# Layer 2's gated feed-forward blocks 5 to 21 as seven half-size products instead of eight

## The chip, the cores and the metric

The kernel runs on one core of a Trainium2 chip. Five engines matter: TensorE (PE) multiplies, with its weight loads shown apart as PEld; VectorE (DVE), ScalarE (ACT) and GpSimd (POOL) work on elements; SyncE (SP) issues the transfers. Each engine takes its instructions in the order in which they stand in its queue. The metric is the device time of the core in microseconds, as the median of several runs.

## The reference

A sequence of 512 tokens with 1024 features passes through two blocks, each with two layers. The change touches only the first block, and there only the second layer (l = 1), whose sublayers are a gated feed-forward (ffn1), a mixer of four kinds of heads, and another gated feed-forward (ffn2). Cut to that:

```python
D_MODEL = 1024; SEQ = 512; DEPTH = 2; D_FF = 2816

def swiglu(h, w13, w2):
    a, b = jnp.split(h @ w13, 2, axis=-1)
    return (jax.nn.silu(a) * b) @ w2

for l in range(DEPTH):
    mod = (cond @ ada_w[l] + ada_b[l]).reshape(B, N_SUBLAYERS, 3, 1, D)
    h = adaln_pre(x, norm_g[l, 0], mod[:, 0, 0], mod[:, 0, 1])
    x = x + 0.5 * mod[:, 0, 2] * swiglu(h, ffn1_w13[l], ffn1_w2[l])
    ...
    h = adaln_pre(x, norm_g[l, 2], mod[:, 2, 0], mod[:, 2, 1])
    x = x + 0.5 * mod[:, 2, 2] * swiglu(h, ffn2_w13[l], ffn2_w2[l])
```

Then the second block (a spatial gating unit, differential attention and a convolutional feed-forward, twice) follows.

## The kernel before

Activations lie with features on the 128 partitions and the 512 tokens along the free axis: the residual is eight tiles `xs[d]` of 128x512. Each float32 operand of a product is split into a rounded part hi (a cast on ACT) and the rest lo (a subtraction), and `mm3` (L397) makes three matmuls of each step: hi by hi, hi by lo, lo by hi.

**Weights.** A list of units, made in the order of use by the planner (`plan_ffn`, L263), is loaded by `load` (L318) into one of three `raw` buffers of 128x2048. `split_one` (L329) turns half a unit (1024 columns, eight steps of K) into a tile `w` of a pool of five: one cast on ACT (L345), then four subtractions of 256 columns on POOL (L348). The products of the adaptive norm (`ada` units) also go through this list, but they are two DVE instructions each (L339, 128x1024). `next_w` (L391) takes a finished tile and calls `pump` (L359), which splits ahead until two tiles are ready. In ffn1 of layer 2, eight ada units stand among blocks 3 to 8: one behind block 3, two behind 4, one behind 5, two behind 6, one each behind 7 and 8. In ffn2 there are none.

**A feed-forward** (`ffn`, L667) has 22 blocks of 128 hidden features. For each block `project` (L717) multiplies twice, gate and value, 24 matmuls of 512 columns each; ACT takes silu of the gate, DVE multiplies by the value out of PSUM (L688), and `hilo` (L412 to L416) splits the result: cast on ACT, lo on DVE. The blocks go in two portions (`HALVES`, L21): after 12 and after the other 10, `out_phase` (L560) multiplies them by w2, eight outputs of 36 or 30 matmuls with two weight tiles each, and `x_add` (L554) adds each output to the residual. The last two outputs of the last portion are joined with the next norm in `seam` (L597), in two halves of the tokens.

PSUM has a pool of five general tiles (`pt`) and three for products (`pd`).

## Time and profile before

| | |
|---|---|
| median of three runs | 3350.55 us (3347.01 to 3351.17) |
| profiled execution, its own time | 3353.2 us |
| its span | 3351.4 us |
| mean granted TensorE clock | 0.989 |
| PE busy | 3252.3 us, 97% |
| DVE, ACT, POOL busy | 46%, 38%, 51% |
| layer 2's ffn1 blocks | from about 1142 us |
| layer 2's ffn2 blocks | from about 1861 us |

The profile is one execution on the chip: start and length of every instruction, what its engine waited for before it, and the chain of work that ended last. Busy shares are averages over the whole span; a single stage is read from the windows, timelines and waits of that stage.

### The profile page before, as it was taken

Reading aid. Unit: us, or ns where it says so; the run is one execution under the profiler, and the core shown is the slowest. Engines: PE = TensorE matmul, PEld = TensorE weight load, DVE = VectorE, ACT = ScalarE, POOL = GpSimd, SP = SyncE. Lnnn points to the kernel's source line nnn. Section 1 sums busy time; section 2 is a strip of 40 time slices with the busy share of each in tenths; the row PEclk is TensorE's granted clock in tenths of the full one; section 3 lists DMA queues with packets and bytes.
Section 4 is the critical chain, followed back from the end, with each engine's and each line's share of the span. In section 5 each row is a group of like instructions: output and inputs, shape, how many; then the busy total and the mean of one; then the engine's idle time right before and its main releaser. Section 6 shows DMA issues by size and latency. Waiting matters only on the chain.

```text
span 3351.4 us, 45142 instructions
## 1 busy us (share of the span) xinstructions
PE 3252.3 (97%) x17498; PEld 2690.2 (80%) x17498; DVE 1531.5 (46%) x2918; ACT 1282.6 (38%) x2127; POOL 1725.9 (51%) x2205
## 2 busy tenths in 40 slices
PE   6999999999999999999999999999999999999998
PEld 4878877678888888887778888887888887788887
DVE  6425377655333421137765221166452437654143
ACT  4222354443222422236344322355442335644242
POOL 5656562135566655556213655554465655355553
PEclk9999999999999999999999999999999999999999
DMA  6546323124454443232202222222132222222322
GB/s 251 196 165 237 113 101 103 64 78 174 167 213 165 145 153 111 78 122 91 91 27 88 101 91 102 81 97 81 64 107 95 96 93 82 67 89 90 107 87 65
DMA packets 72238, 379.18 MB, mean 113 GB/s; under 512 B 7566, under 2 KB 10126, under 8 KB 41560
## 3 DMA queue, kind: packets, MB, share of 16 engines
q1 hardware_dynamic: 72008, 376.28, 32.6%
q8 instruction: 138, 2.26, 0.3%
q14 instruction: 76, 0.62, 0.1%
q10 hardware_dynamic: 16, 0.02, 0.0%
HBM read 369.96 MB, written 6.31 MB: 112 GB/s over the span
## 4 chain that ended last, share of the span: by engine, by line
PE 74%; DVE 5%; ACT 2%; issue 0%; POOL 0%; DMA 0%; DVEq 0%; ACTq 0%; POOLq 0%
PE p L402 21%; PE p L401 21%; PE p L403 21%; PE p L1166 1%; PE p L1541 1%; PE po L1769 1%; PE p L729 1%; PE p L728 1%; PE p L727 1%; PE p L1524 1%; ACT w L345 0%; DVE rt L1639 0%; DVE qk L1640 0%; DVE qk L1641 0%; DVE pp L1749 0%
## 5 line engine op out<-in xcount | busy, mean ns | idle before, releaser
L348 POOL TENSOR_TENSOR w<-raw,w 128x256 fp32r<-128x256 f32 (+1 forms) x2128 | 1687.0, 824 | 1566.2 <-ACT w L345 1418.2
L401 PE MATMUL p<-hi,w 128*128 128x512 f32 (+1 forms) x4400 | 1649.6, 375 | 17.0 <-ACT hi L170 13.3
L402 PE MATMUL p<-lo,w 128*128 128x512 f32 (+1 forms) x4400 | 1640.6, 373 | 2.4 <-DVE lo L485 2.2
L403 PE MATMUL p<-hi,w 128*128 128x512 f32 (+1 forms) x4400 | 1636.2, 372 | 1.0 <-POOL w L383 1.0
L401 PEld LDWEIGHTS p<-hi,w 128*128 128x128 f32 x4400 | 833.2, 189 | 167.5 <-ACT hi L170 16.0
L402 PEld LDWEIGHTS p<-lo,w 128*128 128x128 f32 x4400 | 832.7, 189 | 152.9 <-issue 5.6
L403 PEld LDWEIGHTS p<-hi,w 128*128 128x128 f32 x4400 | 832.4, 189 | 146.2 <-issue 3.9
L345 ACT CAST w<-raw 128x1024 fp32r<-128x1024 f32 (+3 forms) x580 | 552.8, 956 | 866.1 <-PE p L403 725.3
L339 DVE SCALAR_TENSOR_TENSOR raw<-raw,cond 128x1024 f32<-128x1024 f32 x144 | 202.4, 1436 | 188.9 <-DMA raw<-in_ada_dram 181.6
L688 DVE TENSOR_TENSOR s<-s,p 128x512 f32<-128x512 f32 x88 | 60.3, 686 | 398.6 <-PE p L403 394.0
L556 DVE SCALAR_TENSOR_TENSOR x<-p,gate,x 128x512 f32<-128x512 f32 (+1 forms) x92 | 62.5, 679 | 337.1 <-PE p L403 337.1
L416 DVE TENSOR_TENSOR lo<-s,hi 128x512 fp32r<-128x512 f32 x132 | 126.2, 956 | 99.6 <-ACT hi L415 99.5
L696 DVE SCALAR_TENSOR_TENSOR cv<-p,cols,cv 128x511 f32<-128x511 f32 x88 | 65.6, 749 | 209.8 <-ACT cv L170 209.8
L415 ACT CAST hi<-s 128x512 fp32r<-128x512 f32 x132 | 81.6, 618 | 191.5 <-DVE s L688 135.1
L170 ACT ACTIVATE cv<-p,cols 128x512 f32<-128x512 f32 x88 | 68.3, 780 | 211.6 <-PE p L403 211.5
L170 ACT ACTIVATE s<-p 128x512 f32<-128x512 f32 x88 | 52.5, 597 | 212.8 <-PE p L403 212.8
L558 DVE TENSOR_TENSOR x<-p,x 128x512 f32<-128x512 f32 (+1 forms) x56 | 34.4, 615 | 208.2 <-PE p L403 208.2
L431 DVE TENSOR_TENSOR ss<-ss,sq 128x512 f32<-128x512 f32 (+1 forms) x97 | 65.2, 672 | 60.6 <-ACT sq L170 59.7
L170 ACT ACTIVATE sq<-x 128x512 f32<-128x512 f32 (+1 forms) x97 | 52.6, 543 | 101.4 <-DVE x L556 54.7
L170 ACT ACTIVATE pp<-pp,sm 128x128 f32<-128x128 f32 (+3 forms) x128 | 70.9, 555 | 45.1 <-DVE sm L817 34.4
L729 PE MATMUL p<-w,hi 128*128 128x512 f32 (+1 forms) x192 | 73.8, 384 | 4.7 <-POOL w L348 4.7
L727 PE MATMUL p<-w,hi 128*128 128x512 f32 (+1 forms) x192 | 74.4, 388 | 0.0
(401 smaller groups left out, 2450.0 us busy)
## 6 DMA issues: line engine op xcount, KB each, us to landing
raw<-in_ada_dram SPq DMA_DIRECT2D x72, 1024.0 KB, 4.9
raw<-in_f2w_dram SPq DMA_DIRECT2D x44, 1024.0 KB, 4.9
raw<-in_w_up_dram SPq DMA_DIRECT2D x44, 1024.0 KB, 4.8
raw<-in_f1w_dram SPq DMA_DIRECT2D x42, 1024.0 KB, 4.9
raw<-in_w_in_dram SPq DMA_DIRECT2D x36, 1024.0 KB, 4.9
raw<-in_w_out_dram SPq DMA_DIRECT2D x16, 1024.0 KB, 4.9
raw<-in_f1w_dram SPq DMA_DIRECT2D x16, 768.0 KB, 4.2
raw<-in_f2w_dram SPq DMA_DIRECT2D x16, 768.0 KB, 4.3
```

Of the source, the lines that this page charges most:

```text
L170: r = S.activation(dst, src, f, **kw)
L339: V.scalar_tensor_tensor(t[:, j * D : (j + 1) * D], t[:, j * D : (j + 1) * D], 1.0, cond, op0=ALU.mult, op1=ALU.mult, accum_out=mod[:, k : ...
L345: S.copy(w[:, 0, :n], t[:, o : o + n])
L348: P.tensor_sub(w[:, 1, c:e], t[:, o + c : o + e], w[:, 0, c:e].bitcast(F32))
L401: PE.matmul(o[:, sl], wh[:, c], ah[:, sl], start=start, stop=False)
L402: PE.matmul(o[:, sl], wh[:, c], al[:, sl], start=False, stop=False)
L403: PE.matmul(o[:, sl], wl[:, c], ah[:, sl], start=False, stop=stop)
L415: S.copy(hi, src)
L416: V.tensor_sub(lo, src, hi.bitcast(F32))
L696: V.scalar_tensor_tensor(y[:, 1:], p[:, : T - 1], wc(1), y[:, 1:], op0=ALU.mult, op1=ALU.add)
L727: PE.matmul(p[:, :n], h[k][0][:, q], w[0][:, c], start=k == 0, stop=False)
L729: PE.matmul(p[:, :n], h[k][0][:, q], w[1][:, c], start=False, stop=k == 7)
```

## The change

In both gated feed-forwards of layer 2, blocks 0 to 4 stay as they are. For each of the blocks 5 to 21 the block's weights are seen as two by two: a11 and a12 are the gate's weights for the first and the second half of K, a21 and a22 the value's. The right side is two by two as well, halves of K by halves of the tokens. The product is then formed in the manner of Strassen and Winograd by seven products of half the size instead of eight: 7 x 4 steps of K x 3 = 84 matmuls of 128x256, each with a weight load of its own, instead of 48 of 128x512.

- `split_seven` makes the four weight tiles of such a block out of one raw unit. DVE forms s1 = a21 + a22 (L349), a21 = a11 − a21 (L350), a11' = s1 − a11 (L352, over a11) and a12' = a12 − a11' (L359, over a12). All seven of a11, a11', a21, s1, a12, a22 and a12' are split: the casts on ACT, seven of 512 columns (L338); the lo parts of s1 and of a12' on DVE (512 columns, L342), the other five on POOL, two pieces of 256 columns each (L342).
- `seven_rhs` makes the sums of the input halves, for four pairs of K tiles, once per feed-forward, in two portions: two pairs before block 1, two before block 3. A pair costs two additions into PSUM (512 columns, L711), six steps of 256 columns (L714 to L719) and two splits (cast on ACT, lo on DVE).
- `seven` multiplies and combines. The combination is on DVE with one PSUM source, 256 columns (L741 to L760); ACT takes silu in two halves.
- `finish` (L765 to L767: the second half's product with silu, the cast to hi, lo) is issued only in the next block, ahead of its third weight tile, or at the end of the portion.
- Both feed-forwards go in three portions (`THIRDS`: 8, 7 and 7 blocks), so w2 is multiplied in three rounds with one weight tile of 1024 or 896 columns for each output.

```diff
--- before.py
+++ after.py
@@ -19,6 +19,9 @@
...
 HALVES = ((0, 12), (12, 22))
+THIRDS = ((0, 8), (8, 15), (15, 22))
+SEVEN = (('ffn1', 1), ('ffn2', 1))
+SEVEN_FROM = 5
...
@@ -260,17 +263,22 @@
...
-    def plan_ffn(w13, w2, l, ada=None):
+    def plan_ffn(w13, w2, l, ada=None, seven=False):
...
-        for k0, k1 in HALVES:
+        for k0, k1 in THIRDS if seven else HALVES:
             for f in range(k0, k1):
-                if f > 1 or not lead:
+                if seven and f >= SEVEN_FROM:
+                    add_w(w13[l, f], "seven")
+                elif f > 1 or not lead:
                     add_w(w13[l, f], [(0, 1024), (1024, 1024)])
                 if f > (5 if lead else 2) and ada and ada_l[ada[0]] < ada[1]:
                     ada_until(ada[0], min(ada[1], ada_l[ada[0]] + ada[2][f % 2]))
             n = (k1 - k0) // 2 * 128
             for d in range(8):
-                add_w(w2[l, d][:, k0 * 128 : k1 * 128], [(0, n), (n, n)])
+                if seven:
+                    add_w(w2[l, d][:, k0 * 128 : k1 * 128], [(0, (k1 - k0) * 128)])
+                else:
+                    add_w(w2[l, d][:, k0 * 128 : k1 * 128], [(0, n), (n, n)])
...
@@ -280,7 +288,7 @@
...
-            plan_ffn(a["f1w13"], a["f1w2"], l, (l, 36, (2, 1)))
+            plan_ffn(a["f1w13"], a["f1w2"], l, (l, 36, (2, 1)), (st, l) in SEVEN)
...
@@ -298,7 +306,7 @@
...
         if st == "ffn2":
...
-            plan_ffn(a["f2w13"], a["f2w2"], l, (l + 1, 36, (2, 1)) if l + 1 < L else None)
+            plan_ffn(a["f2w13"], a["f2w2"], l, (l + 1, 36, (2, 1)) if l + 1 < L else None, (st, l) in SEVEN)
...
@@ -325,6 +333,34 @@
...
+
+    def split_slab(w, o, src, eng):
+        S.copy(w[:, 0, o : o + 512], src)
+        step = PIECE if eng is P else 512
+        for c in range(0, 512, step):
+            e = slice(o + c, o + c + step)
+            eng.tensor_sub(w[:, 1, e], src[:, c : c + step], w[:, 0, e].bitcast(F32))
+
+    def split_seven(t, i):
+        a11, a12, a21, a22 = (t[:, j * 512 : j * 512 + 512] for j in range(4))
+        w = wsp.tile([128, 2, 1024], R, name="w", tag="w")
+        if i == 0:
+            state["s1"] = s1 = tt("s1")
+            V.tensor_add(s1, a21, a22)
+            V.tensor_sub(a21, a11, a21)
+            split_slab(w, 0, a11, P)
+            V.tensor_sub(a11, s1, a11)
+            split_slab(w, 512, a11, P)
+        if i == 1:
+            split_slab(w, 0, a21, P)
+            split_slab(w, 512, state.pop("s1"), V)
+        if i == 2:
+            split_slab(w, 0, a12, P)
+            V.tensor_sub(a12, a12, a11)
+            split_slab(w, 512, a22, P)
+        if i == 3:
+            split_slab(w, 0, a12, V)
+        return w
     def split_one():
         u = state["u"]
@@ -339,6 +375,10 @@
...
             done = True
+        elif subs == "seven":
+            ready.append(split_seven(t, state["s"]))
+            state["s"] += 1
+            done = state["s"] == 4
         else:
...
@@ -664,12 +704,86 @@
     t5 = {}
-    def ffn(l, sub, gated, h, pre, nxt, first, hook):
-        for hi, (k0, k1) in enumerate(HALVES):
+    def seven_rhs(h, r):
+        for k in range(len(r), len(r) + 2):
+            b = [pt("b"), pt("b")]
+            for j in range(2):
+                V.tensor_add(b[j], h[k + 4 * j][0].bitcast(F32), h[k + 4 * j][1].bitcast(F32))
+            ta, tb = tt("ta"), tt("tb")
+            A, B = SPLIT
+            V.tensor_copy(ta[:, A], b[0][:, A])
+            V.tensor_sub(ta[:, A], b[0][:, B], ta[:, A])
+            V.tensor_sub(ta[:, B], b[1][:, B], ta[:, A])
+            V.tensor_copy(tb[:, A], b[0][:, B])
+            V.tensor_sub(tb[:, A], b[1][:, B], tb[:, A])
+            V.tensor_sub(tb[:, B], b[1][:, A], ta[:, B])
+            r.append((hilo(ta), hilo(tb)))
+
+    def seven(h, t, tail):
+        A, B = SPLIT
+
+        def prod(p, w, o, rhs, start):
+            wh, wl = w
+            for k in range(4):
+                ah, al = rhs(k)
+                c = slice(o + k * 128, o + k * 128 + 128)
+                PE.matmul(p[:, A], wh[:, c], ah, start=start and k == 0, stop=False, skip_group_check=True)
+                PE.matmul(p[:, A], wh[:, c], al, start=False, stop=False, skip_group_check=True)
+                PE.matmul(p[:, A], wl[:, c], ah, start=False, stop=k == 3, skip_group_check=True)
+
+        hk = lambda j, sl: lambda k: (h[k + 4 * j][0][:, sl], h[k + 4 * j][1][:, sl])
+        tk = lambda j, sl: lambda k: (t[k][j][0][:, sl], t[k][j][1][:, sl])
+        m1, m6 = pt("m1"), pd("m6")
+        w = next_w()
+        prod(m1, w, 0, hk(0, A), True)
+        prod(m6, w, 512, tk(0, B), True)
+        u = tt("u2")
+        V.tensor_copy(u[:, A], m1[:, A])
+        V.tensor_add(u[:, A], m6[:, A], u[:, A])
+        m7, m5 = pt("m7"), pt("m5")
+        w = next_w()
+        prod(m7, w, 0, tk(1, A), True)
+        V.tensor_add(u[:, B], m7[:, A], u[:, A])
+        prod(m5, w, 512, tk(0, A), True)
+        V.tensor_add(u[:, B], m5[:, A], u[:, B])
+        if tail:
+            tail.pop()()
+        w = next_w()
+        prod(m1, w, 0, hk(1, A), False)
+        prod(m7, w, 512, tk(1, B), False)
+        s = tt("s")
+        act(s[:, A], m1[:, A], AF.Silu)
+        V.tensor_add(m7[:, A], m7[:, A], u[:, A])
+        w = next_w()
+        prod(m5, w, 0, hk(1, B), False)
+        V.tensor_mul(s[:, A], m7[:, A], s[:, A])
+        V.tensor_add(m5[:, A], m5[:, A], u[:, A])
+        act(s[:, B], m5[:, A], AF.Silu)
+        out = (tt("hi", R), tt("lo", R))
+
+        def finish():
+            V.tensor_mul(s[:, B], s[:, B], u[:, B])
+            S.copy(out[0], s)
+            V.tensor_sub(out[1], s, out[0].bitcast(F32))
+
+        tail.append(finish)
+        return out
+
+    def ffn(l, sub, gated, h, pre, nxt, first, hook, fast=False):
+        parts = THIRDS if fast else HALVES
+        rhs, tail = [], []
+        for hi, (k0, k1) in enumerate(parts):
             nk = k1 - k0
             gs = []
             early = []
             for f in range(k0, k1):
+                if fast and f in (1, 3):
+                    seven_rhs(h, rhs)
+                if fast and f >= SEVEN_FROM:
+                    gs.append(seven(h, rhs, tail))
+                    if f == k1 - 1:
+                        tail.pop()()
+                    continue
                 if first and f == 0:
                     ws = [next_w(j + 1) for j in range(4)]
                     early = [pt() for _ in range(4)]
@@ -705,14 +819,16 @@
...
-            if hi == 0:
-                if gated:
-                    set_gate(l, sub, 0.5)
-                out_phase(2, nk, gs, gated, None)
-                hook()
+            nw = 1 if fast else 2
+            if hi == 0 and gated:
+                set_gate(l, sub, 0.5)
+            if hi < len(parts) - 1:
+                out_phase(nw, nk, gs, gated, None)
+                if hi == 0:
+                    hook()
...
-                h = None
-                return out_phase(2, nk, gs, gated, nxt)
+                h = rhs = None
+                return out_phase(nw, nk, gs, gated, nxt)
...
@@ -1824,9 +1940,9 @@
...
-            h, pre = ffn(l, 0, True, h, pre, nxt, lead and i == 0, hk)
+            h, pre = ffn(l, 0, True, h, pre, nxt, lead and i == 0, hk, (st, l) in SEVEN)
         if st == "ffn2":
-            h, pre = ffn(l, 2, True, h, pre, nxt, False, hk)
+            h, pre = ffn(l, 2, True, h, pre, nxt, False, hk, (st, l) in SEVEN)
...
```

**DVE in ffn1 of layer 2, two steady blocks of the last portion.** Before, a block has two instructions there (s is the gated product, p the value's PSUM tile):

```order
L688 TENSOR_TENSOR s_10965<-s_10965,p_10940 128x512
L416 TENSOR_TENSOR lo_10969<-s_10965,hi_10968 128x512
L688 TENSOR_TENSOR s_11036<-s_11036,p_11011 128x512
L416 TENSOR_TENSOR lo_11040<-s_11036,hi_11039 128x512
L688 TENSOR_TENSOR s_11107<-s_11107,p_11082 128x512
L416 TENSOR_TENSOR lo_11111<-s_11107,hi_11110 128x512
```

After (m are the PSUM products, u the running sum, raw the weights, s_ with a number s1, and L765 and L767 the closing steps):

```order
L760 TENSOR_TENSOR m_11630<-m_11630,u_11626 128x256
L765 TENSOR_TENSOR s<-s,u_11626 128x256
L741 COPY u_11757<-m_11723 128x256
L767 TENSOR_TENSOR lo<-s,hi 128x512
L349 TENSOR_TENSOR s_11797<-raw 128x512
L742 TENSOR_TENSOR u_11757<-m_11724,u_11757 128x256
L350 TENSOR_TENSOR raw<-raw 128x512
L342 TENSOR_TENSOR w<-s_11797,w 128x512
L746 TENSOR_TENSOR u_11757<-m_11760,u_11757 128x256
L352 TENSOR_TENSOR raw<-s_11797,raw 128x512
L748 TENSOR_TENSOR u_11757<-m_11761,u_11757 128x256
L359 TENSOR_TENSOR raw<-raw 128x512
```

Between the combining steps of a block stand the weight sums of the next block, and the closing lo of the block before.

**POOL in ffn1 of layer 2, the weight split.** Before, each tile w is four pieces of one raw buffer:

```order
L348 TENSOR_TENSOR w_10501<-raw_10355,w_10501 128x256 x4
L348 TENSOR_TENSOR w_10546<-raw_10405,w_10546 128x256 x4
L348 TENSOR_TENSOR w_10577<-raw_10405,w_10577 128x256 x4
L348 TENSOR_TENSOR w_10617<-raw_10455,w_10617 128x256 x4
L348 TENSOR_TENSOR w_10648<-raw_10455,w_10648 128x256 x4
```

After, a block is five slabs of two pieces each: a11, a21, a12, a11' and a22; the first row of the next block follows:

```order
L342 TENSOR_TENSOR w_11012<-raw_10713,w_11012 128x256 x2
L342 TENSOR_TENSOR w_11050<-raw_10713,w_11050 128x256 x2
L342 TENSOR_TENSOR w_11075<-raw_10713,w_11075 128x256 x2
L342 TENSOR_TENSOR w_11012<-raw_10713,w_11012 128x256 x2
L342 TENSOR_TENSOR w_11075<-raw_10713,w_11075 128x256 x2
L342 TENSOR_TENSOR w_11146<-raw_10847,w_11146 128x256 x2
```

The first and the fourth row of a block write the same tile, with the pieces of two other tiles between them.

**DVE in ffn1 of layer 2, around block 3.** Before (L339 are the products of the adaptive norm, s and p as above):

```order
L339 SCALAR_TENSOR_TENSOR raw,mod<-raw,cond 128x1024 x4
L688 TENSOR_TENSOR s<-s,p 128x512
L416 TENSOR_TENSOR lo<-s,hi 128x512
L339 SCALAR_TENSOR_TENSOR raw,mod<-raw,cond 128x1024 x4
L688 TENSOR_TENSOR s<-s,p 128x512
L339 SCALAR_TENSOR_TENSOR raw,mod<-raw,cond 128x1024
L416 TENSOR_TENSOR lo<-s,hi 128x512
L339 SCALAR_TENSOR_TENSOR raw,mod<-raw,cond 128x1024 x2
L688 TENSOR_TENSOR s<-s,p 128x512
L339 SCALAR_TENSOR_TENSOR raw,mod<-raw,cond 128x1024
L416 TENSOR_TENSOR lo<-s,hi 128x512
```

After (L375 is what L339 was, L802 what L688 was; L456 is the lo of ta and tb, the input sums, and of s):

```order
L456 TENSOR_TENSOR lo<-ta,hi 128x512
L456 TENSOR_TENSOR lo<-tb,hi 128x512
L802 TENSOR_TENSOR s<-s,p 128x512
L456 TENSOR_TENSOR lo<-s,hi 128x512
L349 TENSOR_TENSOR s_9637<-raw 128x512
L375 SCALAR_TENSOR_TENSOR raw,mod<-raw,cond 128x1024
L350 TENSOR_TENSOR raw<-raw 128x512
L342 TENSOR_TENSOR w<-s_9637,w 128x512
L352 TENSOR_TENSOR raw<-s_9637,raw 128x512
L375 SCALAR_TENSOR_TENSOR raw,mod<-raw,cond 128x1024
L359 TENSOR_TENSOR raw<-raw 128x512
L342 TENSOR_TENSOR w<-raw,w 128x512
```

The first seven-product block's weight sums (L349, L350, L352, L359 and two lo) stand behind the last of the input sums and between products of the adaptive norm.

## Rows read from the trace of the kernel before

**Rows 1.** The page: busy time by engine, and the chain that ended last.
```profile
PE 3252.3 (97%) x17498; PEld 2690.2 (80%) x17498; DVE 1531.5 (46%) x2918; ACT 1282.6 (38%) x2127; POOL 1725.9 (51%) x2205
...
PE 74%; DVE 5%; ACT 2%; issue 0%; POOL 0%; DMA 0%; DVEq 0%; ACTq 0%; POOLq 0%
```

**Rows 2.** Windows in layer 2's ffn2: length, then busy time by engine.
```profile
core 0: us, PE busy (x) PEld busy (x) DVE busy (x) ACT busy (x) POOL busy (x), PEclk, DMA share, GB/s
1865.00:1975.00 110.00, 110.00 (x487) 91.09 (x486) 15.16 (x20) 30.16 (x40) 63.89 (x85) 1.00 0.29 97
1986.00:2050.00 64.00, 64.00 (x284) 53.01 (x283) 11.34 (x16) 15.07 (x18) 37.64 (x53) 1.00 0.33 112
```

**Rows 3.** The chain of waits from 1986 to 2050, by line.
```profile
by line: PE p L403 33.6%; PE p L401 33.3%; PE p L402 33.3%
```

**Rows 4.** Timeline of PE, 512 columns: start, length, engine, line, operation.
```profile
1900.29 0.39 PE L401 MATMUL p<-hi,w 128*128 128x512 f32 x1
...
1903.01 0.39 PE L401 MATMUL p<-hi,w 128*128 128x512 f32 x1
```

**Rows 5.** Timeline of PE, 256 columns.
```profile
1840.05 0.28 PE L403 MATMUL p<-hi,w 128*128 128x256 f32 x1
...
1841.13 0.28 PE L403 MATMUL p<-hi,w 128*128 128x256 f32 x1
```

**Rows 6.** Timeline of POOL: four pieces of a weight tile.
```profile
1900.39 3.28 POOL L348 TENSOR_TENSOR w<-raw,w 128x256 fp32r<-128x256 f32 x4 [2.27 <-ACT w L345]
1906.18 2.82 POOL L348 TENSOR_TENSOR w<-raw,w 128x256 fp32r<-128x256 f32 x4 [2.52 <-ACT w L345]
```

**Rows 7.** Timelines of DVE and ACT beside those pieces.
```profile
1900.87 0.81 DVE L416 TENSOR_TENSOR lo<-s,hi 128x512 fp32r<-128x512 f32 x1 [0.97 <-ACT hi L415]
...
1905.07 1.04 ACT L345 CAST w<-raw 128x1024 fp32r<-128x1024 f32 x1
```

**Rows 8.** Durations: two lines by source, then groups by form.
```profile
L701 DVE TENSOR_TENSOR s<-s,cv x44: 692/1154/1257, 2432.1 to 3286.9; 128x512 f32<-128x512 f32 x44
...
L688 DVE TENSOR_TENSOR s<-s,p x88: 675/687/699, 57.6 to 2149.4; 128x512 f32<-128x512 f32 x88
...
L1171 DVE TENSOR_TENSOR gE<-p,cst 128x256 f32<-128x256 f32 x40 | 16.6, 418 | 17.8 <-PE p L1166 17.3
...
L415 ACT CAST hi<-s 128x512 fp32r<-128x512 f32 x132 | 81.6, 618 | 191.5 <-DVE s L688 135.1 <-DVE s L701 56.4
...
L170 ACT ACTIVATE ab<-p 128x256 f32<-128x256 f32 x8 | 3.1, 384 | 47.0 <-PE p L1350 47.0
```

**Rows 9.** DVE in layer 2's ffn1: timeline, and groups from 1140 to 1206.
```profile
1146.63 1.22 DVE L339 SCALAR_TENSOR_TENSOR raw<-raw,cond 128x1024 f32<-128x1024 f32 x1 [2.67 <-issue]
...
1204.73 0.69 DVE L416 TENSOR_TENSOR lo<-s,hi 128x512 fp32r<-128x512 f32 x1 [0.69 <-ACT hi L415]
1207.48 0.69 DVE L688 TENSOR_TENSOR s<-s,p 128x512 f32<-128x512 f32 x1 [2.06 <-PE p L403]
1209.15 1.13 DVE L416 TENSOR_TENSOR lo<-s,hi 128x512 fp32r<-128x512 f32 x1 [0.98 <-ACT hi L415]
1218.36 0.69 DVE L688 TENSOR_TENSOR s<-s,p 128x512 f32<-128x512 f32 x1 [8.08 <-PE p L403]
...
L339 DVE SCALAR_TENSOR_TENSOR raw<-raw,cond 128x1024 f32<-128x1024 f32 x16 | 22.3, 1420 | 24.7 <-DMA raw<-in_ada_dram 22.0 <-issue 2.7
```

**Rows 10.** Timeline of PE at an FFN's seam and at the mixer's.
```profile
1495.09 0.28 PE L403 MATMUL p<-hi,w 128*128 128x256 f32 x1
1495.49 0.67 PE L446 MATMUL rp<-ss,ones 128*128 128x256 f32 x2
...
1845.07 0.28 PE L403 MATMUL p<-hi,w 128*128 128x256 f32 x1
1846.15 0.70 PE L446 MATMUL rp<-ss,ones 128*128 128x256 f32 x2 [0.80 <-DVE ss L431]
```

## The prediction, made before the changed kernel ran

> **What bounds the kernel now.** I read the page's shares first, then the stretches of the blocks at stake by windows, then the chain of waits in one of them. TensorE is busy 97% of the span and holds 74% of the chain that ended last [rows 1]. In two stretches of layer 2's ffn2 (1865 to 1975 are ten blocks, 1986 to 2050 is for the most part its w2 products) PE is busy for the whole window, 110.00 of 110.00 and 64.00 of 64.00 us, at a granted clock of 1.00 (the 2.4 GHz level); DVE has 15.16 of 110 there, ACT 30.16, POOL 63.89 [rows 2]. The chain of the second holds the three matmul lines alone, a third each [rows 3]. So a block costs what its matmuls cost, and everything else hides: room to add DVE and ACT work, as long as it doesn't become a chain longer than the block.
>
> **The matmuls.** A 512-column matmul follows the last after (1903.01 − 1900.29) / 12 = .2267 us [rows 4]; a block's 48 take 10.88, which the block spacing on DVE confirms (1218.36 − 1207.48 = 10.88 [rows 9]). A 256-column matmul, each with its own weight load, follows after (1841.13 − 1840.05) / 9 = .120 [rows 5]: not half, but 53%. Seven products of 4 x 3 such steps are 84 x .120 = 10.08. Gain .80 a block, and 17 blocks in each of two FFNs: **−27.2 us**. That is the most the change can give.
>
> The Trainium skill ("TensorE: Matmul & The Clock Gate", section "Back-to-back issue gap") gives N/2.4 + 2.5 ns for an isolated warm matmul: by it 109 and 216 ns, 1.2 us a block and about −40. The rows are 120 and 227 ns; the measurement decides.
>
> **What is added to the other engines.** Per block the weight split had two casts of 1024 on ACT and eight 256-column pieces on POOL, nothing on DVE, and DVE had two operations, s*p (.687) and lo (.69 to 1.13) [rows 8, 9]. Now ACT has seven casts of 512 (.618 each, 4.3), two silu of 256 columns (.384, taken from ACT's 256-column read of PSUM) and the hi cast (.618): 5.7 of 10.08, fits. POOL has ten pieces at 2.82 / 4 = .70 [rows 6]: 7.0, fits. DVE has six 512-column operations with two SBUF inputs (.69), seven 256-column ones with a PSUM input (.418), one from SBUF (.42) and lo (.69): 8.2, fits alone. Shares say that it hides. What decides is the order: DVE, ACT and POOL hand the same weights round.
>
> **How DVE and POOL stand to each other.** Four pieces take 2.82 with DVE quiet, 3.28 with one DVE lo (two SBUF inputs) starting inside them [rows 6, 7]: +.46 of POOL time, for an operation of .69. The gating product of two SBUF tensors takes 692 ns at best, 1154 in the median, while the product with PSUM stays at 675 to 699 [rows 8]. So an operation with two SBUF inputs and a POOL piece take turns; a turn of both costs 1154 rather than .70 + .69. I split it: sub .55 after the piece, piece .60 after the sub.
>
> **The loop.** In the steady order one block's weight operations and the last block's closing steps form one ring, which comes back to the same instruction one block later. From the a12 subtract (L359) of one block to that of the next, in the order of the queues:
> the subtract itself .55; POOL's second a11' piece and first a22 piece, 1.20, while ACT casts the result (.62 + .07 hop [rows 7]) and DVE's lo stands behind a piece; that lo (L342) .55; L759 and L760 behind it in DVE's queue, .70; silu on ACT .44; L765 .45; hi cast with hop .67; lo of L767 .73; s1 (L349) .61; L742 .35; the a21 subtract (L350) .61; its cast .67; POOL's two a21 pieces with L352 between them 1.96; two a12 pieces 1.38, which L359 must wait for since it overwrites a12; and one a11' piece that takes the port first, .69.
> Sum **11.56 us a turn**, more than 10.08 and more than the 10.88 of before. Each turn beyond 10.08 is a PE wait of 1.48 for a weight tile, once the lead is used up. Two blocks' tiles are prepared during the w2 steps ahead; at the first turn the tile is ready about 1.6 before it is wanted (wanted 11.52 after the block's start, ready near 9.95). A portion of seven blocks has five turns: 5 x 1.48 − 1.6 = 5.8. Four such portions (two in each FFN): **+23.2**. The first portions have three seven-product blocks and are counted apart.
>
> **First portion of ffn1.** There DVE also has the adaptive-norm products, 1420 ns on average in this stretch, from 1146.63, when their data lands [rows 9]. DVE's queue from there to block 5's L352 holds five sums b (.8), twenty-four 256-column steps (.45), twelve lo (.8), four s*p (.68), nine of those products (1.42), four weight operations (.8) and .5 of small ones: 4.0 + 10.8 + 9.6 + 2.7 + 12.8 + 3.2 + .5 = 43.6, so 1190.1. POOL, whose queue has a11' behind a21, a12 and a22, gets a21 near 1189.7 and needs eight pieces: 1195.3 to 1195.5. PE has done block 4 at 1185.3 (s*p of block 6 starts at 1207.48 now; less two blocks and the .4 of a matmul's end [rows 9]) and wants a11' 1.44 later, after 12 matmuls: 1186.7. **+9**. With the products at their 1.22 alone and 512 operations at .69 it is +4, with 1.74 and 1.15 it is +15. This is the one stall that doesn't depend on the loop.
>
> **Other parts.** First portion of ffn2, no such products: one turn over the lead, **+1.2** (0 to 2.3). Seams: the last portion's out phase now holds one w2 tile per output, as the mixer's does, whose seam lets PE wait .80 where the FFN's waits near nothing (1846.15 after 1845.07, against 1495.49 after 1495.09 [rows 10]): **+.7** for two, 0 to 1.4. The end of a portion: m5's last matmul, L760 .42, silu .39, L765 .42, hi .62, lo .69 and hops are 2.9 to 3.4, covered by the six or seven other blocks' w2 steps, at least 6 x 3 x .227 = 4.1: 0 (to .5 each, were it uncovered by a late DVE). Eight more residual adds per FFN at .7 lie under 21 or 24 matmuls each: 0. A third more w2 transfers, smaller ones; DMA share is .29 to .33 in rows 2: 0.
>
> **Sum** −27.2 + 23.2 + 9 + 1.2 + .7 = +6.9. The profiled execution took 3353.2 with a span of 3351.4; against it 3360; against the median of the runs, 3350.55, **3357.5**. 0.2% (6.7 us) is about what can be told from no change here.
>
> **Rivals.**
> A, the ring hides and the kernel is faster: no port turn falls into it. Then the three places where I counted a piece or sub more than its own .69 (1.20, 1.96, the .69 ahead of L359) shrink by .51, .58 and .69, with the subs at .69 instead of .55: 10.06 a turn, just inside 10.08. Left are −27.2 + 9 + .3 + .7: 3333. For it: the gating product's minimum is 692. Against: its median is 1154. It decides from a turn of 10.4 downwards, since the lead of 1.6 covers five turns of .32 over.
> B, in between, a turn of 10.4 to 11.2: at 10.88, 5 x .8 − 1.6 = 2.4 a portion, 9.6 in all, so near 3344 (3334 to 3350). POOL's pieces could be done just ahead of two of the three places.
> C, slower by far: each of the ring's two-input operations waits for a whole piece. s1 (L349), L350 and L767 stand where I let POOL be idle; +.46 at each makes 12.9 a turn, 5 x 2.8 − 1.6 = 12.5 a portion, 50 in all: about 3385. With it at one of them alone, a turn of 12.0, 3366 and still the forecast's; at two, 12.5, near 3376.
> D, the 256-column matmul isn't .120 where DVE and ACT read PSUM beside it; 10.88 / 84 = .1295 is break-even: by that alone the −27.2 is gone, and with the stalls unhidden under the longer block about 3362.
>
> The Trainium skill ("SBUF — State Buffer", on the DVE-GpSimd shared port pair) says that the pair is an exclusive lock for a whole instruction, held by a DVE operation with two SBUF inputs against a GpSimd one that reads SBUF. The rows agree on who collides and on 1154; a little less than the full 1.39 is paid. Were the full lock paid (+.14 at some nine turns of the port) the ring would be 12.8 and the time as C's.
>
> **How the numbers follow.** Forecast (turn 11.2 to 11.9, ffn1's first portion +4 to +15, so 3345 to 3371): .45, of which .20 within 0.2% and .25 slower. A .22, faster. B .10, .05 faster and .05 same. C .20, slower. D .03, slower. Together faster .27, same .25, slower .48. The range 3333 to 3379 leaves about a tenth at each end.
>
> **What would show it.** Right: PE gaps of about 1.5 us once a block from the third seven-product block of a portion on, ended by POOL or DVE w; block spacing 11.4 to 11.7; one gap of some 9 us near 1186, with DVE busy without a break from 1147. Wrong: spacing of 10.08 with no gap (A); spacing above 12.5 with DVE's L349, L350 and L767 at 1.1 and more (C); matmuls apart by other than .120 (D); ffn1's first portion without a gap, if DVE's sums start earlier than the order lets me believe.

## The result, and the profile after

The changed kernel takes 3392.68 us (median of four runs, 3387.66 to 3396.61) against 3349.85 for the kernel before: ratio 1.0136, interval 1.0121 to 1.0152 (the two medians alone give 1.0128). That is 42.8 us slower by the medians, where 3357.5 was forecast and 3379 was the upper end. The profiled execution took 3388.97 with a span of 3386.9.

Section 1 of the page of the profile, answering to [rows 1]: PE is still busy 96% of a longer span, DVE went from 1531.5 to 1853.0 us.

```profile
PE 3239.5 (96%) x18686; PEld 2727.5 (81%) x18686; DVE 1853.0 (55%) x3456; ACT 1364.2 (40%) x2331; POOL 1814.0 (54%) x2273
```

The windows of the two feed-forwards of layer 2, each from the seam ahead of it to its own. The columns are the length, the busy time of PE, PEld, DVE, ACT and POOL (with the number of instructions), then the granted clock, the DMA share and GB/s. First before:

```profile
1122.50:1485.30 362.80, 362.53 (x1720) 305.10 (x1720) 88.91 (x140) 109.66 (x153) 207.53 (x272) 1.00 0.36 124
1836.40:2198.80 362.40, 361.55 (x1708) 303.75 (x1708) 78.04 (x123) 109.44 (x153) 199.34 (x268) 1.00 0.28 94
```

and after:

```profile
1115.30:1507.00 391.70, 364.30 (x2333) 330.57 (x2333) 248.22 (x409) 150.96 (x256) 253.55 (x310) 0.98 0.35 117
1855.90:2234.50 378.60, 359.36 (x2321) 326.45 (x2321) 240.11 (x392) 151.24 (x256) 248.29 (x306) 0.99 0.29 94
```

The stretches grew by 28.9 and 16.2 us. Of each, 1.9 is only the window's edge: with shorter last portions, matmuls move from behind the own seam's start to ahead of it, and in the run with the three portions alone, which costs nothing (below), the same stretches are 364.7 and 364.3 us. From the first seam to the end the execution took 2271.6 (3386.9 − 1115.3) against 2228.9 (3351.4 − 1122.5), so 42.7: the whole difference lies here, and the 7 us by which the stretch starts earlier come from layer 1, which the change doesn't touch: up to there the granted clock stands at .50 for 23.9 us in this trace, for 37.6 in the trace before. Two things stand in these rows. PE now idles 27.4 and 19.2 us where it idled .3 and .9. And its busy time, 723.7 in the two together, is what it was (724.1), although 34 blocks were to take .80 less each: busy time was added too, and the clock column (.98 and .99, before 1.00) says by what for a part of it.

What PE waited for, in ffn1 and then in ffn2 (us in total, times, longest):

```profile
PE m L730 <- DVE u L746: 11.1, 9, 1.2
PE m L732 <- POOL w L342: 3.7, 1, 3.7
PE p L441 <- DVE s L802: 3.3, 1, 3.3
PE m L730 <- DVE u L741: 3.1, 2, 2.7
PE p L441 <- ACT hi L766: 2.5, 3, 1.2
PE p L442 <- DVE lo L767: 2.1, 3, 0.8
PE m L730 <- DVE u L748: 1.2, 2, 0.7
PE rp L486 <- DVE ss L471: 0.2, 1, 0.2
...
PE m L730 <- DVE u L746: 10.9, 10, 1.3
PE p L441 <- ACT hi L766: 5.6, 3, 3.2
PE p L442 <- DVE lo L767: 1.6, 3, 0.7
PE rp L486 <- DVE ss L471: 0.8, 1, 0.8
```

Three groups. **L746**, 22.0 us in nineteen waits (one of them in ffn1's first portion), is the ring. **L342, L802, L741 and L748**, 11.3 us, all lie in ffn1's first portion. **hi L766 and lo L767**, 11.8 us, are the six ends of portions. The seams ahead of the two stretches (L486) have 1.0, as in the kernel before (.2 and .8). The seams that the change touches stand just behind the windows: PE waits .39 and .60 us at 1513.18 and 1516.49, and .64 at 2243.63, where no wait is over .15 before.

**The ring.** PE's timeline at two successive blocks of ffn1's second portion, against [rows 5]:

```profile
1299.98 0.28 PE L732 MATMUL m<-hi,w 128*128 128x256 f32 x1
1301.49 0.39 PE L730 MATMUL m<-hi,w 128*128 128x256 f32 x1 [1.23 <-DVE u L746]
...
1311.63 0.28 PE L732 MATMUL m<-hi,w 128*128 128x256 f32 x1
1313.14 0.39 PE L730 MATMUL m<-hi,w 128*128 128x256 f32 x1 [1.23 <-DVE u L746]
```

A turn is 11.65 us (1313.14 − 1301.49), of which 1.39 is the gap beyond the .120 step. DVE in the same block, and what its weight sums take over all blocks (min/median/max in ns), against [rows 8]:

```profile
1302.49 0.41 DVE L748 TENSOR_TENSOR u<-m,u 128x256 f32<-128x256 f32 x1
1304.60 1.21 DVE L359 TENSOR_TENSOR raw<-raw 128x512 f32<-128x512 f32 x1 [1.70 <-POOL w L342]
...
L359 DVE TENSOR_TENSOR raw<-raw x34: 1194/1210/1218, 1186.3 to 2184.6; 128x512 f32<-128x512 f32 x34
```

L359 waits 1.70 for POOL's a12 pieces and then takes 1.21 instead of .69, while POOL starts on a piece of a11'.

**An end of a portion.** ACT, then DVE, then PE, at the end of ffn1's second portion:

```profile
1349.77 0.94 ACT L385 CAST w<-raw 128x896 fp32r<-128x896 f32 x1 [1.94 <-DMA raw<-in_f1w_dram]
1352.26 0.95 ACT L385 CAST w<-raw 128x896 fp32r<-128x896 f32 x1 [1.55 <-DMA raw<-in_f1w_dram]
1353.11 0.38 ACT L173 ACTIVATE s<-m 128x256 f32<-128x256 f32 x1
1354.23 0.62 ACT L766 CAST hi<-s 128x512 fp32r<-128x512 f32 x1 [0.75 <-DVE s L765]
...
1350.14 0.43 DVE L760 TENSOR_TENSOR m<-m,u 128x256 f32<-128x256 f32 x1 [0.48 <-PE m L732]
...
1354.90 0.49 PE L441 MATMUL p<-hi,w 128*128 128x512 f32 x1 [0.69 <-ACT hi L766]
1356.07 0.50 PE L442 MATMUL p<-lo,w 128*128 128x512 f32 x1 [0.67 <-DVE lo L767]
```

The portion's last silu stands in ACT's queue behind two casts of w2 tiles, which wait for their transfers. DVE had given it its input (L760) at 1350.58; it starts at 1353.11.

**The clock.** PE after the wait of 3.27 at the start of ffn1's block 3 (the expectations below count it to block 2), then the window of three microseconds in it, and last a window of 52 us with four of the ring's waits:

```profile
1159.81 0.50 PE L441 MATMUL p<-hi,w 128*128 128x512 f32 x1 [3.27 <-DVE s L802]
1160.14 0.39 PE L442 MATMUL p<-lo,w 128*128 128x512 f32 x1
...
1161.60 0.63 PE L441 MATMUL p<-hi,w 128*128 128x512 f32 x1
1162.03 0.63 PE L442 MATMUL p<-lo,w 128*128 128x512 f32 x1
...
1164.48 0.39 PE L442 MATMUL p<-lo,w 128*128 128x512 f32 x1
1164.70 0.39 PE L443 MATMUL p<-hi,w 128*128 128x512 f32 x1
...
1161.00:1164.00 3.00, 3.00 (x8) 2.35 (x8) 3.00 (x4) 0.00 (x0) 1.61 (x2) 0.50 0.13 25
...
1292.00:1344.00 52.00, 47.07 (x383) 46.12 (x383) 40.05 (x66) 23.54 (x45) 39.63 (x48) 1.00 0.19 60
```

A microsecond after PE resumes, a 512-column matmul follows the last after .43 us instead of .227, at a granted clock of .50 (the 1.2 GHz level), until 1164.2. There are six such stretches in the two feed-forwards, 20 us in all: behind the waits of 3.27 and 2.66 in ffn1's first portion, from the end of the one of 3.68 there, and behind the end of ffn1's last portion and those of ffn2's second and last (1.24 + .79, 3.15 + .22 and 1.36 + .69). Behind the ring's waits and the other three ends (.54 + .67, .69 + .67 and 1.11 + .67) there are none. The longer steps in the six add 9.6 us. The other steps that are longer, short of a listed wait, add 7.5 us to those of before, at a granted clock of 1.00: about half are the first two steps after each wait (1301.49 to 1301.72 is .23 instead of .120), and why these are longer the trace doesn't show; the rest is for the most part waits too short to be listed.

### The profile page after: what moved, and what is told of

It reads as the page before. It is cut to its first block, busy times and chain, and to the rows that moved or that the text cites. A ratio compares the mean times of both kernels' runs of the same rounds, so it can differ in the third digit from the quotient of the medians.

```text
span 3386.9 us, 48609 instructions
## 1 busy us (share of the span) xinstructions
PE 3239.5 (96%) x18686; PEld 2727.5 (81%) x18686; DVE 1853.0 (55%) x3456; ACT 1364.2 (40%) x2331; POOL 1814.0 (54%) x2273
## 5 line engine op out<-in xcount | busy, mean ns | idle before, releaser
L388 POOL TENSOR_TENSOR w<-raw,w 128x256 fp32r<-128x256 f32 (+1 forms) x1856 | 1485.5, 834 | 1337.7 <-ACT w L385 1190.5
L441 PE MATMUL p<-hi,w 128*128 128x512 f32 (+1 forms) x3844 | 1436.5, 374 | 28.8 <-ACT hi L173 13.7
L442 PE MATMUL p<-lo,w 128*128 128x512 f32 (+1 forms) x3844 | 1429.2, 372 | 6.6 <-DVE lo L767 3.7
L443 PE MATMUL p<-hi,w 128*128 128x512 f32 (+1 forms) x3844 | 1422.7, 370 | 0.5 <-POOL w L423 0.5
L441 PEld LDWEIGHTS p<-hi,w 128*128 128x128 f32 x3844 | 729.1, 190 | 160.3 <-ACT hi L173 16.2
L443 PEld LDWEIGHTS p<-hi,w 128*128 128x128 f32 x3844 | 728.1, 189 | 124.9 <-issue 3.5
L385 ACT CAST w<-raw 128x1024 fp32r<-128x1024 f32 (+4 forms) x496 | 478.6, 968 | 662.0 <-PE p L443 497.0
L342 POOL TENSOR_TENSOR w<-raw,w 128x256 fp32r<-128x256 f32 x340 | 289.2, 887 | 175.4 <-ACT w L338 102.2
L730 PE MATMUL m<-hi,w 128*128 128x256 f32 x952 | 275.3, 289 | 26.8 <-DVE u L746 22.0
L375 DVE SCALAR_TENSOR_TENSOR raw<-raw,cond 128x1024 f32<-128x1024 f32 x144 | 202.0, 1431 | 157.7 <-DMA raw<-in_ada_dram 150.6
L732 PE MATMUL m<-hi,w 128*128 128x256 f32 x952 | 270.5, 284 | 3.7 <-POOL w L342 3.7
L731 PE MATMUL m<-lo,w 128*128 128x256 f32 x952 | 270.3, 284 | 0.0
L730 PEld LDWEIGHTS m<-hi,w 128*128 128x128 f32 x952 | 183.3, 193 | 34.2 <-DVE u L746 28.1
L338 ACT CAST w<-raw 128x512 fp32r<-128x512 f32 x204 | 118.0, 618 | 178.6 <-DVE raw L359 69.6
L732 PEld LDWEIGHTS m<-hi,w 128*128 128x128 f32 x952 | 183.5, 193 | 3.9 <-POOL w L342 3.9
L731 PEld LDWEIGHTS m<-lo,w 128*128 128x128 f32 x952 | 183.5, 193 | 0.2
L456 DVE TENSOR_TENSOR lo<-s,hi 128x512 fp32r<-128x512 f32 x98 | 99.7, 1017 | 63.9 <-ACT hi L455 63.7
```

The lines of the kernel that those rows point to most:

```text
L338: S.copy(w[:, 0, o : o + 512], src)
L342: eng.tensor_sub(w[:, 1, e], src[:, c : c + step], w[:, 0, e].bitcast(F32))
L375: V.scalar_tensor_tensor(t[:, j * D : (j + 1) * D], t[:, j * D : (j + 1) * D], 1.0, cond, op0=ALU.mult, op1=ALU.mult, accum_out=mod[:, k : ...
L385: S.copy(w[:, 0, :n], t[:, o : o + n])
L388: P.tensor_sub(w[:, 1, c:e], t[:, o + c : o + e], w[:, 0, c:e].bitcast(F32))
L441: PE.matmul(o[:, sl], wh[:, c], ah[:, sl], start=start, stop=False)
```

## The experiments

All make small edits to the changed kernel; times are medians, each beside runs of the kernel before on the same chip. That kernel took 3346.0 us beside four of the runs (copy on ACT, closing steps not deferred, order at the portions' ends, adaptive-norm units) and 3349.4 to 3349.8 beside the others. So where a run is compared with the changed kernel, its distance from its own kernel before is set against 42.8.

**Seven products in ffn2 alone.**

```diff
-SEVEN = (('ffn1', 1), ('ffn2', 1))
+SEVEN = (('ffn2', 1),)
```

> Only layer 2's ffn2 is changed; ffn1 is as before. In the changed kernel's trace the stretch from seam to seam is 391.7 us in ffn1 (362.8 before) and 378.6 in ffn2 (362.4 before): +28.9 and +16.2. If the two are separate, this is 14 to 18 us slower than before, near 3366. If what the profile lost in ffn2 comes from ffn1's lateness (loads, tiles), it is within 5 us of before.

Measured: 3362.7 (3358.7 to 3364.2), ratio 1.0040 (1.0025 to 1.0054), so 13.3 us over before, a little under what I expected; without the 1.9 of the window's edge the stretch had grown by 14.3. ffn2 costs this by itself; by difference, ffn1 brings the rest of the 42.8.

**The three portions alone.**

```diff
-SEVEN_FROM = 5
+SEVEN_FROM = NF
-                if fast and f in (1, 3):
+                if fast and SEVEN_FROM < NF and f in (1, 3):
```

> The three portions alone, with one weight tile for each w2 output, in both feed-forwards of layer 2; all 22 blocks are two products as before. Theory A, the waits at the ends of the portions (1.0 to 3.8 us each, six ends, some 14 in all) come from the seven-product block's longer closing chain and its late start: here every end is covered, and only the two seams and residual adds are left, 0 to +3 us on before. Theory B, they come from w2 transfers that land late since each output now takes a whole raw buffer: the waits stand here too, +8 to +15.

Measured: 3351.1, ratio 1.0007 (.9997 to 1.0016). Theory A: three w2 rounds with one tile for each output cost nothing that can be told, and no end of a portion makes PE wait, in ffn1 or in ffn2.

**a12' in a tile of its own.**

```diff
-            V.tensor_sub(a12, a12, a11)
+            state["c"] = c = tt("c")
+            V.tensor_sub(c, a12, a11)
...
-            split_slab(w, 0, a12, V)
+            split_slab(w, 0, state.pop("c"), V)
```

> The changed kernel, with a12' written into a tile of its own, so that L359 no longer overwrites a12 and needn't wait for POOL's two a12 pieces; the same arithmetic. Ring theory: in the changed kernel's trace L359 starts at 1304.60, when POOL's second a12 piece ends (1304.56), though DVE has been free since 1302.90. Without that wait the turn of 11.65 loses about 1.7 and comes to 9.9 to 10.3, so the block spacing to 10.1 to 10.4; of 4 x 5.7 us of PE waits in the portions of seven 3 or less each at most stay, with the half clock behind them: 18 to 26 us faster than the changed kernel, 3367 to 3375. Load theory (DVE has simply too much to do beside POOL in such a block): spacing stays above 11.3, less than 6 us faster.

Measured: 3380.2 (3379.2 to 3387.3), ratio 1.0098 (1.0082 to 1.0114), 30.8 over before: 12 us faster than the changed kernel, not 18 to 26. The turn fell from 11.65 to 10.8 and the gap from 1.39 to .44, so the wait on a12 was in the ring; but another ring, of 10.8, stood right behind it. DVE in one of its blocks (L360 is the a12 subtract, L766 and L768 the closing product and lo), then PE's longest waits, two lines of ffn1 and one of ffn2:

```profile
1330.51 0.90 DVE L360 TENSOR_TENSOR c<-raw 128x512 f32<-128x512 f32 x1
...
1334.05 0.78 DVE L766 TENSOR_TENSOR s<-s,u 128x256 f32<-128x256 f32 x1 [0.45 <-ACT s L173]
1334.75 0.41 DVE L742 COPY u<-m 128x256 f32<-128x256 f32 x1
1335.52 1.16 DVE L768 TENSOR_TENSOR lo<-s,hi 128x512 fp32r<-128x512 f32 x1 [0.35 <-ACT hi L767]
...
PE m L733 <- POOL w L342: 9.7, 3, 4.4
PE p L442 <- ACT hi L767: 7.1, 3, 3.4
...
PE p L442 <- ACT hi L767: 9.0, 3, 3.4
```

DVE works without a break but for .45 and .35, when it waits for ACT. The load theory, which I had given 11.3 and more, was the second bound, only lower. The other half of what I missed is that the waits moved on: with the lo (1.1) the ends of portions are 17.2 us here instead of 11.8, the waits for POOL's w 11.3 (1.6 in ffn2) instead of 3.7, and the longer steps at half clock 20.0 instead of 9.6. This profiled execution is the slowest of the four, 7 us over their median.

**The copy of m1 on ACT.** As the run before, with

```diff
-        V.tensor_copy(u[:, A], m1[:, A])
+        S.copy(u[:, A], m1[:, A])
```

> As the run with a12' in a tile of its own, and the copy of m1 to u (L741, .41 us) on ACT instead of DVE. In that run the turn was 10.77, with DVE busy nearly without a break (waits of .44 at block after block). If DVE's own row of work is now the ring, the turn loses .33 and comes to 10.4 to 10.5, the waits of .44 go to .1 or less, and the time is 3 to 8 us under that run's 3380. If POOL and the port are the ring, the turn stays at 10.7 to 10.8 and the time within 2 us.

Measured: 3385.1 (3378.4 to 3386.0), ratio 1.0119 (1.0102 to 1.0136), 39.1 over before, 8 more than the last run: no gain. The turn stays at 10.8. This did not show POOL as the ring, as I had expected of such a result. DVE's row tells why:

```profile
1329.68 1.16 DVE L768 TENSOR_TENSOR lo<-s,hi 128x512 fp32r<-128x512 f32 x1 [0.69 <-ACT hi L767]
```

The copy had filled the wait for the hi cast (.35 above, .69 here). What was taken from DVE was already hidden.

**Closing steps not deferred.** `finish()` is called where it is defined, and the two places that pop it later are gone.

> The changed kernel with one part undone: a block's closing steps (L765 to L767) are issued at the block's end, not in the next block. Ring theory: DVE then stands idle while ACT casts hi, and the copy L741, which fills that time in the changed kernel, comes after; the turn grows by about .33 from 11.65 to 12.0, the wait from 1.39 to 1.7, with five turns in each of four portions 5 to 8 us slower than the changed kernel. Rival: deferring only frees L767 from the chain, and nothing changes (within 2 us).

Measured, in one run: 3409.5, 63.5 over before, so 21 us slower than the changed kernel, with a turn of 13.0. The direction is the ring theory's, but the turn grew by 1.35 where I gave it .33: PE now waits for L741 too (1.5 us a block), which stands behind the lo that waits for the cast. Deferring was worth 1.3 us a block.

**POOL's pieces of 512 columns.**

```diff
-        step = PIECE if eng is P else 512
+        step = 512
```

> The changed kernel, with POOL's lo slabs of a seven-product block in one instruction of 512 columns instead of two of 256. If a DVE operation with two SBUF inputs waits for the POOL instruction under way as a whole, L359 waits for twice as long a piece and the turn grows by .4 to .7 from 11.65, to 12.1 to 12.3: 8 to 14 us slower than the changed kernel. If the two share the port evenly in time, the pieces' width doesn't matter: the turn stays at 11.5 to 11.7.

Measured, in one run: 3380.9, 31.1 over before. The turn is 11.62, as if the port were shared in time; but the durations say the opposite:

```profile
L359 DVE TENSOR_TENSOR raw<-raw x34: 1734/1766/1771, 1188.9 to 2177.3; 128x512 f32<-128x512 f32 x34
```

A DVE operation with two SBUF inputs did wait for the whole POOL instruction (1.77 instead of 1.21, beside a piece of 1.30 instead of .75). The turn didn't grow since there were half as many encounters, and L359 waited 40.4 / 34 = 1.2 us ahead of its start, where 65.5 / 34 = 1.9 before. My mechanism held and my sum for it didn't. The time is 12 us under the changed kernel's all the same. In the traces the two stretches are 8.6 us shorter, and 6.0 of that is less half clock (longer steps of 3.6 instead of 9.6); whether this comes from the edit, one execution doesn't show.

**The order at the portions' ends.**

```diff
-            S.copy(w[:, 0, :n], t[:, o : o + n])
+            r = S.copy(w[:, 0, :n], t[:, o : o + n])
+            if last["n"]:
+                after(r.ins, [last["n"]])
...
-            S.copy(out[0], s)
+            last["n"] = S.copy(out[0], s).ins.name
```

> The changed kernel, with one order forced on ACT: a w2 tile's cast (L385) may not stand ahead of the hi cast (L766) of a block's closing steps that the code issues before it. In the changed kernel's queue two such casts stand ahead of a portion's last silu, and in its trace they wait for their transfer (1.94 and 1.55 us at 1349.77 and 1352.26), so that silu starts at 1353.11 instead of some 1350.6. Queue theory: the waits at the ends of the six portions (1.66, 1.79 and 2.48 in ffn1, 2.22, 3.81 and 2.48 in ffn2: 14.4) fall to 3 in all, and some 6 us of half clock behind them go too: 14 to 22 us faster than the changed kernel, 3371 to 3379. Transfer theory (the w2 transfers are simply late): the waits move to a later w2 output, less than 5 us faster.

Measured: 3367.8 (3366.1 to 3370.1), ratio 1.0067 (1.0052 to 1.0082), 21.8 over before: 21 us faster than the changed kernel, at the upper end of what I expected. ACT at the end of ffn1's second portion, and all that PE waited for from 1330 to 1400:

```profile
1348.69 0.39 ACT L173 ACTIVATE s<-m 128x256 f32<-128x256 f32 x1 [2.96 <-DVE m L763]
1349.56 0.62 ACT L769 CAST hi<-s 128x512 fp32r<-128x512 f32 x1 [0.49 <-DVE s L768]
1350.09 1.78 ACT L386 CAST w<-raw 128x896 fp32r<-128x896 f32 x2
...
PE m L733 <- DVE u L749: 1.2, 1, 1.2
```

Silu now waits for DVE, the casts come after, and the one wait left is a ring's. The waits at all six ends are gone, and with them the three stretches of half clock behind them; those in ffn1's first portion stay (longer steps of 6.0 instead of 9.6). The transfers were late, but only a queue's order made them matter.

**ffn1's adaptive-norm units among the w2 tiles.** In `plan_ffn` such units are skipped in blocks of a seven-product feed-forward, and one is added behind each w2 unit of the first portion.

> The changed kernel, with ffn1's eight adaptive-norm units moved from blocks 3 to 8 to among the first portion's w2 tiles, one behind each. Theory: ffn1's first portion waits 14.4 us since DVE has these products (some 1.4 us each, sixteen) beside the input sums; without them the wait of 3.4 at block 2 and the 3.8 at block 5 go to under 1 each, and some of the 7 us in blocks 5 to 7: 9 to 15 us faster than the changed kernel, 3378 to 3384. Rival: the input sums alone, or the ring, hold DVE: the waits stay within 4 us of 14.4.

Measured: 3382.9 (3376.0 to 3387.5), ratio 1.0110 (1.0091 to 1.0128), 36.9 over before: 6 us faster than the changed kernel, under the 9 to 15 that I expected, and the two intervals touch; in the traces, from the first seam on, it is 5. In ffn1's first portion the waits for L802 and for POOL's a11' are gone but for .2; PE waits 5.2 us there instead of 12.5. Some of it came back: the waits at four later ends of portions are now 3.3 us each, where one was.

**Seven products from block 8 on.**

```diff
-SEVEN_FROM = 5
+SEVEN_FROM = 8
```

> Seven products only from block 8 on (14 blocks in each feed-forward): the first portion has none, the input sums stay at blocks 1 and 3. Ledger of the changed kernel: ffn1's first portion waits 14.4 us and runs 3.2 us longer at half clock, of which 3.4 + 1.6 stand at block 2, behind the input sums, and stay. Lost are 2 x 3 x .8 = 4.8 us of matmul gain. So 7 to 12 us faster than the changed kernel, 3381 to 3386, and no wait of over 1 us between 1165 and 1225. Rival: the first portion's lateness moves on to block 8, and the time is within 4 us of the changed kernel's.

Measured: 3373.9 (3371.8 to 3377.1), ratio 1.0074 (1.0057 to 1.0091), 24.5 over before: 18 us faster than the changed kernel (14 in the traces) although six blocks fewer have the cheaper product. That is more than I expected. One wait of 1.5 that I did not expect stands at 1185.8, for s*p (L802) behind the second pairs of input sums. Also gone are the waits at the ends of the two first portions, 3.0 us. The first portion's seven-product blocks cost more than they gave.

**The three edits together.** Own tile, casts behind the closing cast, adaptive-norm units moved.

> The three edits that each took a term away, together: a12' in a tile of its own, w2 casts behind the closing hi cast, and ffn1's adaptive-norm units among the first portion's w2 tiles. Ledger: 3367.8 with the casts' order alone; the ring's waits in the four portions of seven fall from 22.9 to some 5.4 (17 less), the first portion's from 14 to 6 (8 less, and 2 of half clock). If the terms add up, 3367.8 - 27 = 3341, 3337 to 3346, which is 0 to 0.4% under before. If they hide one another (the ring takes back what the first portion gives) it stays above 3350.

Measured: 3343.57, ratio .9989 (.9980 to .9998), 49 us under the changed kernel: the terms add up.

**Closing steps among the next weight sums.** As the last, with L765 made to follow the next L349 in DVE's queue, L767 the next L350; for this a block's third weight tile is taken before the closing steps are issued.

> As the run of three edits, and a block's closing product (L765) put behind the next s1 (L349) in DVE's queue, its lo (L767) behind the next a21 subtract (L350). In the run with a12' in its own tile the turn was 10.8, and DVE stood idle in it for .45 until silu and for .69 until the hi cast, with the copy L741 in the second of these: this is why the copy's move to ACT changed nothing. Theory: DVE's own row of work with these two idle times is now the ring; filled, the turn comes to 10.1 or less, the waits of .44 go, and it is 4 to 9 us faster than the three edits. Rival: POOL and the port are the ring (ten pieces with their waits take 10 us): within 2 us of the three edits.

Measured: 3343.62, ratio .9985 (.9976 to .9994): no gain. The turn did fall, from 10.8 to 10.5, but not to 10.1, and what the turns saved went into half clock: the longer steps there are 6.5 us in the two stretches instead of 3.1. What holds 10.5, as far as this trace shows, is the POOL of the rival theory, which now works through a turn but for .19:

```profile
1305.11 10.28 POOL L345 TENSOR_TENSOR w<-raw,w 128x256 fp32r<-128x256 f32 x10 [0.19 <-POOL w L345]
```

The ten pieces take 1.03 each here, beside DVE, where four took .70 each with DVE quiet [rows 6]. No run takes work from POOL to try this.

**Three edits, and ffn1 from block 8.**

> As the run of three edits, and in ffn1 seven products only from block 8 on (ffn2 from block 5 as there). In that run ffn1's first portion still has waits of 1.69, .53, .32, 3.09, 1.10 and .87 us (7.6) around the first seven-product blocks, with some 2 us of half clock. If they come from starting the ring while the input sums still hold DVE, they go, for 3 x .8 = 2.4 of matmul gain: 6 to 8 us faster than the 3343.6 of the three edits, 3335 to 3338, which is .4% under before. If they only move to block 8, within 3 us of 3343.6.

Measured: 3337.23 (3332.97 to 3341.79), ratio .9965 (.9952 to .9977), 12 us faster than the kernel before, and as expected. Its windows of the two feed-forwards, as above:

```profile
1120.20:1478.10 357.90, 355.96 (x2224) 322.28 (x2224) 231.59 (x370) 144.59 (x238) 249.90 (x304) 1.00 0.38 128
1826.90:2183.90 357.00, 352.94 (x2321) 324.36 (x2321) 239.38 (x392) 150.98 (x256) 252.11 (x306) 1.00 0.30 100
```

PE idles 2 and 4 us, the clock is back at 1.00, and the seven products, in 31 blocks now, give 12 of the 24.8 us that .80 a block would be; the turns of 10.8 and the waits that are left take the rest.

## Why the prediction was wrong, by its own steps

- **The matmuls, −27.2.** Right: between its waits a block's steps are .120 apart, and a turn without the wait's 1.39 and the .18 of longer steps after it is 10.08.
- **The ring, 11.56 a turn, +23.2.** The mechanism was right, and the size near: 11.65, with the listed steps in that order in the trace and none off by more than .4. From start to start, as the prediction counted, a turn costs 1.57 beyond 10.08 and the four portions 28.1 (19.9 of listed waits). The a12 wait was shown by taking it away. What PE waits for was named wrongly: not a weight tile, but L746. The third tile adds to m7's PSUM, which DVE must have read first, and L746 stands in DVE's queue behind the ring's operations.
- **ffn1's first portion, +9.** Near in sum, and that in part by luck: 11.3 of listed waits, 14.1 from start to start. The one stall of 9 that I forecast, for the late a11', measured 3.7 at block 5. I left out that the input sums also hold up s*p of block 1 (3.3), and that the ring's first turns in blocks 5 to 7 wait for L741 and L748 (4.3).
- **ffn2's first portion +1.2, seams +.7.** 1.5 and 1.6: near.
- **A portion's end, 0.** This step failed: 11.8 us of listed waits, 14.4 from start to start. I added up the closing chain's own durations, 2.9 to 3.4, and found them covered; I didn't look at what stands ahead of silu in ACT's queue, and rows 2's DMA share was read as "transfers hide". (The w2 transfers are half more, 24 in each feed-forward instead of 16, and not a third.) The runs with three portions alone and with the casts' order show the cause: the casts of w2 tiles that wait for transfers, in front of a silu that nobody else can replace.
- **The clock, not in the sum.** This was the other failure: 9.6 us. The forecast took each wait at its length. In this kernel's rows six waits are paid for again right after, at the 1.2 GHz level, as the changed kernel's window of 3 us shows, and that there is such a price could have been read before. The kernel before has no waits in its blocks, but one of 5.75 in its mixer, and the rows behind it show the same steps of .43:

```profile
1564.56 2.08 PE L1110 MATMUL p<-sq,blk 128*128 128x512 f32 x2 [5.75 <-ACT sq L170]
...
1567.28 0.63 PE L403 MATMUL p<-hi,w 128*128 128x512 f32 x1
1567.71 0.63 PE L401 MATMUL p<-hi,w 128*128 128x512 f32 x1
```

I looked only at the stretches that the change touches.

Together, with each matmul counted from the start of the one before it, less its own .120 or .2267: −27.2 for the products, 28.1 for the ring, 14.1 and 1.5 for the first portions, 14.4 for the ends and .9 for longer steps behind them, 9.6 for half clock, 1.6 for the seams. That is +43.0, against 42.7 in the traces, where the forecast had +6.9. Of the 36 us between them the ends are 15 and half clock 10; the ring and ffn1's first portion, right in their mechanism or near it, were each 5 too small. Rival C's number, 3385, came near it by another road: its turn of 12.9 was not seen.

## What to carry to other kernels

When a change turns one engine's stretch from the bound into one of a ring, add up the ring in queue order (the turn held to 1%), and then walk every engine's queue ahead of the last instruction of each stage: a cast that waits for a transfer in front of a short closing step makes that step as late as the transfer. Price a new wait of PE of some microseconds above its length, since what follows can run at half clock for a while (9.6 us behind six waits here). And a saving of 7% in products is worth taking only where the start and end of each portion are clean: the same products gave +43 us and, after four small edits, the last of which took three blocks back to eight products, −12.

## What the hardware showed beyond expectation

After PE's wait of 3.27 us its steps were .43 apart from about 1160.8 to 1164.2, beginning only a microsecond after work had resumed; after the ring's waits of 1.23 only the next step or two were longer (.23 instead of .120), at a granted clock of 1.00. A DVE operation with two SBUF inputs (.69 alone) took 1.21 beside POOL pieces of .75 and 1.77 beside pieces of 1.30: the whole piece, less about .2. The Trainium skill ("SBUF — State Buffer", section "SBUF: two separate sides", on the DVE-GpSimd port pair) has the lock for a whole instruction; the two durations agree with it, but for the .2.
